# A hybrid decoder layer: where the attention heads' merge operands and softmax sums are loaded

## Chip, cores and metric

The kernel runs on one core of a Trainium2 chip, in one launch. The metric is the device time of one execution in microseconds (us). Engines are named as in the profile: PE is TensorE, DVE VectorE, ACT ScalarE, POOL GpSimd, SP SyncE, which issues most of the DMAs.

## The reference

One layer on x of 1 x 1024 x 1024 in float32: a half-step SwiGLU FFN, a mixer of two branches, a second half-step FFN, a final norm. Only the end of the mixer matters here:

```python
o_dn = rmsnorm(gated_delta_rule(...), dn_out_norm) * silu(dn_z)      # branch A, 8 heads of 128
# branch B: 8 heads; each query keeps its top-256 causal keys
logits = q_lat . c_sel * 128**-0.5 + rel_bias                        # masked
p = softmax(logits)
o_sa = (p . c_sel) @ w_uv                                            # per head, 128 wide
merged = sigmoid(gate_a) * o_dn + sigmoid(gate_b) * o_sa
x = x + merged @ w_o
```

## The kernel before

Every product is made of three matmuls on split operands (`mm3`, lines 139 to 141): a value is cast to a high part and the rest is kept as a low part (line 111 casts on ScalarE, line 112 subtracts on VectorE or GpSimd). The matrices are float32r, the tokens stand in eight blocks of 128.

Before the attention, the delta-rule stage writes its normed output, transposed per head, to `odd` in DRAM, and the gates are written to `zgd` (branch A's gate times silu of z) and `gbd` (the tanh of branch B's gate). In the attention stage `attn_head` runs for eight heads. Per head it goes through four groups g in the order 0, 1, 3, 2, each with two query blocks. For a block it makes the logits (`pl`), adds a mask or a near-bias tile `nb` made on GpSimd (line 1309) while it takes the maximum `a_mx` on VectorE (line 1322), and exponentiates on ScalarE (line 1327), which also gives the row sums `a_sum`. Then the probabilities are transposed on TensorE (`pp`), split into `ph` and `plo` (lines 1338, 1339), and multiplied with the values `vh`, `vl` into the one PSUM bank `pao`; ScalarE copies that into `osa` (line 1344).

After group 1 and after group 2 a half of the head (512 queries) is complete and `merge` is called. It takes the reciprocal of the sums (line 1364), issues three loads from SP (`od`, `zg`, `gb`, line 1369, one buffer each), writes the reciprocals to DRAM (`a_rd`, line 1378) and loads them back spread over all partitions (`a_rb`, line 1380, also SP, which waits there until `a_rd` has landed). The second part of the merge, `done`, multiplies `od` by `zg` on GpSimd (1383), `osa` by `a_rb` and by 1 + `gb` on VectorE (1384, 1385) and adds both into `merged` on GpSimd (1386). It is held back in the list `outs`: for the half after group 1 until the end of group 3, for the half after group 2 until the end of the next head's group 1. `issue_after(dve.ins)` puts its VectorE instructions behind the last `plo` of that group.

`ahead` in group 1 makes the next head's queries and keys (`attn_qk`, line 1288 casts, 1289 subtracts, tile `p`) at a raised priority. `attn_values` makes the values of a pair of heads every second head, in one tile `vh` and one `vl`, from the weights `w_uv`. All weight loads share the two slots of `w_raw`, which are free again when ScalarE has cast and GpSimd has subtracted (tile `wa`).

The order of the instructions on each engine is found by a list scheduler at build time, which takes the ready instruction of the highest priority, by the order of the program unless `high_priority` raises it; each engine and each DMA queue then runs its own list in order. The tiles of a tag share its buffers (`bufs`), and an instruction that writes a buffer waits for the readers of the tile before.

Of the kernel before, what the change touches and what calls it, by code (L numbers as in the profile page):

```python
# [10 lines left out]
F32 = mybir.dt.float32  # L11
F32R = mybir.dt.float32r
# [3 lines left out]
ALU = mybir.AluOpType  # L16
# [4 lines left out]
P = 128  # L21
D = 1024
S = 1024
NK = D // P
NT = S // P
D_FF = 2816
NF = D_FF // P
H = 8
# [42 lines left out]
class Layer:  # L71
# [1188 lines left out]
    def attn_values(self, pair, p, ps):  # L1260
        nc = self.nc
        wh, wl = self.attn_weights(self.I["w_uv"][0][:, 2 * pair:2 * pair + 2, :].rearrange("r h d -> r (h d)"), 256, p, "wuv")
        vh = p.tile([P, NT, 256], F32R, name="vh", tag="vh", bufs=1)
        vl = p.tile([P, NT, 256], F32R, name="vl", tag="vl", bufs=1)
        for t in range(0, NT, 2):
            pv = ps.tile([P, 2, 256], F32, name="pav", tag="qk")
            for i in range(2):
                for k in range(2):
                    lh, ll = (x[2 + k][t // 4][:, ts((t + i) % 4, P)] for x in self.lat)
                    self.mm3(pv[:, i, :], lh, ll, wh[:, k, :], wl[:, k, :], k == 0, k == 1)  # L1270
            nc.scalar.copy(vh[:, t:t + 2, :], pv)
            nc.vector.tensor_sub(vl[:, t:t + 2, :], pv, vh[:, t:t + 2, :])
        return vh, vl

    def attn_qk(self, hd, p, ps):
# [19 lines left out]
    def attn_head(self, hd, p, ps, qk, values, merged, ahead):  # L1295
        nc = self.nc
        near = self.near_tile(p, hd)
        (qh, ql), (kh, kl) = qk
        vh, vl = values
        hv = slice((hd % 2) * P, (hd % 2) * P + P)  # L1300
        sums = self.stat.tile([P, NT], F32, name="a_sum")
        osa = p.tile([P, S], F32, name="osa", tag="osa", bufs=2)
        for g in (0, 1, 3, 2):
            probs = []
            for b in (2 * g, 2 * g + 1):
                W = (b + 1) * P
                n_near = min(W, 256)
                nb = p.tile([P, 256], F32, name="nb", tag="nb", bufs=4)
                nc.gpsimd.tensor_add(nb[:, 256 - n_near:], near[:, 256 - n_near:], self.mask[b][:, W - n_near:W])
                s = self.slot(("w_hi", "w_lo")[b % 2])  # L1310
                mx = self.stat.tile([P, 4], F32, name="a_mx", tag="a_mx", bufs=3)
                m = 0
                for n0 in range(0, W, 512):
                    n1 = min(W, n0 + 512)
                    pl = ps.tile([P, 512], F32, name="pl", tag="lg")
                    self.mm3(pl[:, 0:n1 - n0], qh[b // 4][:, ts(b % 4, P)], ql[b // 4][:, ts(b % 4, P)], kh[n0 // 512][:, 0:n1 - n0],
                             kl[n0 // 512][:, 0:n1 - n0], True, True)
                    for a0, a1 in ((n0, min(n1, W - n_near)), (max(n0, W - n_near), n1)):
                        if a1 <= a0:
                            continue  # L1320
                        add = nb[:, a0 - W + 256:a1 - W + 256] if a0 >= W - n_near else self.mask[b][:, a0:a1]
                        nc.vector.tensor_tensor_reduce(s[:, a0:a1], pl[:, a0 - n0:a1 - n0], add, 1.0,
                                                       mx[:, m - 1:m] if m else -3.0e38, ALU.add, ALU.max, accum_out=mx[:, m:m + 1])
                        m += 1
                nm = self.stat.tile([P, 1], F32, name="a_nm", tag="a_nm", bufs=3)
                nc.vector.tensor_scalar_mul(nm, mx[:, m - 1:m], -1.0)
                nc.scalar.activation(s[:, 0:W], s[:, 0:W], AF.Exp, bias=nm, accum_out=sums[:, b:b + 1])
                probs.append(s)
            po = ps.tile([P, 512], F32, name="pao", tag="ao")
            for j in range(0, 2 * g + 2, 2):  # L1330
                pt = ps.tile([P, 512], F32, name="pp", tag="pt")
                blocks = [(j, 0), (j, 1), (j + 1, 0), (j + 1, 1)] if j < 2 * g else [(j, 0), (j, 1), (j + 1, 1)]
                n = len(blocks) * P
                for i, (jj, b) in enumerate(blocks):
                    nc.tensor.transpose(pt[:, ts(i, P)], probs[b][:, ts(jj, P)], self.ident)
                ph = p.tile([P, 512], F32R, name="ph", tag="ph", bufs=3)
                pl_ = p.tile([P, 512], F32R, name="plo", tag="plo", bufs=3)
                nc.scalar.copy(ph[:, 0:n], pt[:, 0:n])
                dve = nc.vector.tensor_sub(pl_[:, 0:n], pt[:, 0:n], ph[:, 0:n])
                for i in range(2):  # L1340
                    a, b = (0, 256) if i == 0 else (256, n)
                    out = po[:, 0:256] if b - a == 256 else po[:, 128:256]
                    self.mm3(out, vh[:, j + i, hv], vl[:, j + i, hv], ph[:, a:b], pl_[:, a:b], j + i == 0, j + i == 2 * g + 1)
            nc.scalar.copy(osa[:, ts(g, 256)], po[:, 0:256])
            if g == 1:
                ahead()
            for late in self.outs:
                late[0] -= 1
            while self.outs and self.outs[0][0] == 0:
                with self.tc.issue_after(dve.ins):  # L1350
                    self.outs.pop(0)[1]()
            if g in (1, 2):
                out = self.merge(hd, g // 2, sums, osa, p, ps, merged)
                if hd == H - 1 and g == 2:
                    out()
                else:
                    self.outs.append([g, out])

    def merge(self, hd, h, sums, osa, p, ps, merged):


        nc = self.nc
        r = self.stat.tile([P, 4], F32, name="a_r")
        nc.vector.reciprocal(r, sums[:, ts(h, 4)])
        nc.vector.tensor_scalar_mul(r, r, 0.5)
        od, zg, gb = (p.tile([P, 512], F32, name=n, tag=n, bufs=1) for n in ("od", "zg", "gb"))
        v = ts(h, 512)
        for x, src in ((od, self.odd[hd][:, v]), (zg, self.zgd[hd][:, v]), (gb, self.gbd[hd][:, v])):
            nc.sync.dma_start(x, src)
        if hd == H - 1 and h == 1:  # L1370
            rb = ps.tile([P, 512], F32, name="a_rp", tag="pt")
            for t in range(4):
                d = p.tile([P, P], F32, name="a_d", tag="near", bufs=2)
                nc.vector.tensor_scalar_mul(d, self.ident, r[:, t:t + 1])
                nc.tensor.matmul(rb[:, ts(t, P)], lhsT=self.ones, rhs=d, start=True, stop=True)
        else:
            rd = self.dram.tile([512], F32, name="a_rd", tag="a_rd", bufs=2)
            nc.sync.dma_start(rd.rearrange("(t i) -> i t", i=P), r)
            rb = p.tile([P, 512], F32, name="a_rb", tag="a_rb", bufs=1)
            nc.sync.dma_start(rb, rd.partition_broadcast(P))  # L1380

        def done():
            nc.gpsimd.tensor_mul(od, od, zg)
            nc.vector.tensor_mul(osa[:, v], osa[:, v], rb)
            nc.vector.scalar_tensor_tensor(osa[:, v], gb, 1.0, osa[:, v], ALU.add, ALU.mult)
            nc.gpsimd.tensor_add(merged[:, v], od, osa[:, v])

        return done


    def out_proj(self, m, ps, after_tile, after_half):
# [137 lines left out]
    def mixer(self, hs):  # L1529

        nc = self.nc
        ms = ExitStack()
        with ExitStack() as km:
            keep = self.pool(km, "keep", 1)
            self.masks(keep)
            with ExitStack() as ss:
                ps = Banks(self.psum, g=(0, 1), u=(2, 3), t=(4, 5, 6, 7), d=(4, 5, 6, 7))
# [29 lines left out]
                with ExitStack() as c2:  # L1567
                    sp = self.pool(c2, "blocks", 1)
                    blocks = [self.solve_blocks(k, sp, ps) for k in range(2)]
                    with ExitStack() as c3:  # L1570
                        p = self.pool(c3, "qkv", 1)
# [26 lines left out]
                ps = Banks(self.psum, g=(0,), u=(2,), pq=(4, 5), pv=(1, 3), pn=(6, 7), po=(1, 3), qk=(0, 2))  # L1598
# [14 lines left out]
            with ExitStack() as c:  # L1613
                ps = Banks(self.psum, qk=(0, 1), lg=(2, 4, 5), pt=(6, 7), ao=(3,))
                p = self.pool(c, "attn", 1)
                mlp = self.pool(c, "merged_raw", 1)
                raw = [mlp.tile([P, S], F32, name=f"mr{k}", tag=f"mr{k}") for k in range(NK)]
                qk = self.qk

                def ahead():  # L1620
                    if len(qk) < H:
                        with self.tc.high_priority(offset=AHEAD):
                            qk.append(self.attn_qk(len(qk), (p, "wqk", 2), ps))

                for i in range(H):
                    if i % 2 == 0:
# [58 lines left out]
```

## Time and profile before

| | us |
|---|---|
| median of 3 runs | 2654.05 (2652.68 to 2655.29) |
| profiled execution, its own time | 2654.08 |
| its span in the trace | 2652.1 |
| TensorE matmuls busy | 2519.1 (95%) |
| VectorE, ScalarE, GpSimd busy | 1737.9, 1198.3, 970.9 |

Times in the trace are counted from the start of the span; the attention stage lies between about 1600 and 1880 us. The granted clock is the share of TensorE's full clock that the chip granted, as a mean over a stretch. "Idle before" or a wait is the time for which an engine's next instruction was held, put down to the work that released it; "issue" means that the profile shows no releaser. The chain of waits follows back, from the last instruction of a stretch, what released each step. "To landing" is the time from the issue of a DMA to its completion. SPq is SP's queue, PEld TensorE's weight loads.

### The profile page before, as it was taken

The numbers are of one execution on the slowest core, as the hardware profiler recorded it, in microseconds if no ns is written. First come the engines' busy times: TensorE is split into PE (matmuls) and PEld (weight loads), VectorE is DVE, ScalarE is ACT, GpSimd is POOL, SyncE is SP. The second block draws the span as 40 slices with busy tenths as digits, with TensorE's granted clock in tenths as the row PEclk, the third lists the DMA queues.
The fourth block names the chain that finished last, engine by engine and source line by source line (L and its number), as shares of the span: only waits on it lengthen the run. The fifth ranks groups of instructions, "written<-read, shape, count | busy, mean of one in ns | idle before, by whom it ended". The sixth has DMA issues, their size and how long they took to land.

```text
span 2652.1 us, 36132 instructions
## 1 busy us (share of the span) xinstructions
PE 2519.1 (95%) x12526; PEld 2054.9 (77%) x12526; DVE 1737.9 (66%) x3424; ACT 1198.3 (45%) x2338; POOL 970.9 (37%) x748
## 2 busy tenths in 40 slices
PE   6999999999999899989999999779898999999998
PEld 5788888888787688777778778678776888888886
DVE  7655555676555677999566866566668555546676
ACT  6444344333434665544368446445434434434333
POOL 5555444343434233332100002333446545543340
PEclk8999999999999899999999999889998999999999
DMA  5443346753444155445633323333632344347642
GB/s 168 136 143 129 113 146 219 255 194 101 120 114 122 41 140 139 115 124 123 200 124 116 124 82 74 82 76 78 200 111 94 102 143 143 127 150 263 224 151 75
DMA packets 375607, 356.67 MB, mean 134 GB/s; under 512 B 95417, under 2 KB 279553, under 8 KB 374401
## 3 DMA queue, kind: packets, MB, share of 16 engines
q1 hardware_dynamic: 371840, 348.60, 42.1%
q10 hardware_dynamic: 2304, 4.20, 0.4%
q0 software_dynamic: 1280, 1.57, 0.3%
q8 instruction: 99, 1.62, 0.3%
q14 instruction: 84, 0.68, 0.1%
HBM read 238.28 MB, written 116.01 MB: 134 GB/s over the span
## 4 chain that ended last, share of the span: by engine, by line
PE 40%; DVE 9%; DMA 6%; issue 2%; ACT 1%; POOL 1%; SPq 0%; DVEq 0%; POOLq 0%; ACTq 0%
PE pst L139 7%; PE pst L141 7%; PE pst L140 7%; PE pin L141 2%; PE pin L139 2%; PE pin L140 2%; DVE sb_p L1034 2%; DMA a_rd<-a_r 2%; DMA od<-odd 1%; PE pn L1221 1%; PE po L1230 1%; PE pv L1216 1%; DVE cv_y L923 1%; PE pq L1211 1%; PE pwo L141 1%
## 5 line engine op out<-in xcount | busy, mean ns | idle before, releaser
L140 PE MATMUL pst<-p,w_hi 128*128 128x512 f32 x992 | 392.1, 395 | 8.6 <-DVE p L112 8.5
L139 PE MATMUL pst<-p,w_hi 128*128 128x512 f32 x992 | 393.2, 397 | 4.1 <-ACT p L111 2.3
L141 PE MATMUL pst<-p,w_hi 128*128 128x512 f32 x992 | 391.3, 395 | 0.5 <-DVE w_hi L112 0.5
L139 PE MATMUL pin<-p,w_hi 128*128 128x512 f32 (+1 forms) x848 | 342.1, 405 | 6.0 <-DVE cv_y L923 4.2
L111 ACT CAST w_hi<-w_raw 128x512 fp32r<-128x512 f32 (+3 forms) x294 | 204.1, 695 | 311.7 <-PE pst L141 135.8
L140 PE MATMUL pin<-p,w_hi 128*128 128x512 f32 (+1 forms) x848 | 340.5, 402 | 0.5 <-DVE p L112 0.5
L141 PE MATMUL pin<-p,w_lo 128*128 128x512 f32 (+1 forms) x848 | 340.8, 402 | 0.0
L112 DVE TENSOR_TENSOR w_lo<-w_raw,w_lo 128x512 fp32r<-128x512 f32 (+1 forms) x196 | 188.3, 963 | 167.2 <-ACT w_lo L111 165.6
L140 PE MATMUL pst<-p,w_lo 128*128 128x512 f32 x744 | 292.7, 394 | 3.7 <-DVE p L112 3.7
L141 PE MATMUL pst<-p,w_lo 128*128 128x512 f32 x744 | 292.2, 393 | 1.2 <-DVE w_lo L112 1.2
L139 PE MATMUL pst<-p,w_lo 128*128 128x512 f32 x744 | 290.6, 396 | 0.5 <-ACT c L360 0.5
L140 PEld LDWEIGHTS pst<-p,w_hi 128*128 128x128 f32 x992 | 188.3, 190 | 53.9 <-DVE p L112 12.9
L139 PEld LDWEIGHTS pst<-p,w_hi 128*128 128x128 f32 x992 | 188.8, 190 | 47.3 <-ACT p L111 3.5
L141 PEld LDWEIGHTS pst<-p,w_hi 128*128 128x128 f32 x992 | 188.5, 190 | 43.0 <-DVE w_hi L112 1.3
L111 ACT CAST w_lo<-w_raw 128x512 fp32r<-128x512 f32 (+1 forms) x200 | 115.7, 582 | 207.4 <-PE pst L141 97.8
L139 PEld LDWEIGHTS pin<-p,w_hi 128*128 128x128 f32 (+1 forms) x848 | 161.6, 191 | 42.7 <-DVE cv_y L923 4.5
L141 PEld LDWEIGHTS pin<-p,w_lo 128*128 128x128 f32 (+1 forms) x848 | 161.5, 190 | 37.7 <-issue 3.8
L140 PEld LDWEIGHTS pin<-p,w_hi 128*128 128x128 f32 (+1 forms) x848 | 161.6, 191 | 37.5 <-issue 4.0
L373 DVE TENSOR_TENSOR c<-c,pst 128x512 f32<-128x512 f32 x132 | 89.9, 682 | 150.9 <-PE pst L141 118.1
L112 POOL TENSOR_TENSOR w_lo<-w_raw,w_hi 128x1024 fp32r<-128x1024 f32 (+1 forms) x43 | 107.0, 2488 | 199.4 <-ACT w_hi L111 189.4
L140 PEld LDWEIGHTS pst<-p,w_lo 128*128 128x128 f32 x744 | 140.7, 189 | 35.1 <-DVE p L112 4.9
L141 PEld LDWEIGHTS pst<-p,w_lo 128*128 128x128 f32 x744 | 140.7, 189 | 33.5 <-DVE w_lo L112 2.1
(427 smaller groups left out, 5393.8 us busy)
## 6 DMA issues: line engine op xcount, KB each, us to landing
p<-mixd SPq DMA_DIRECT2D x144, 256.0 KB, 5.4
w_raw<-in_w_in_dram SPq DMA_DIRECT2D x52, 512.0 KB, 4.1
w_raw<-in_ffn_wg_dram SPq DMA_DIRECT2D x44, 512.0 KB, 3.6
w_raw<-in_ffn_wu_dram SPq DMA_DIRECT2D x44, 512.0 KB, 4.0
mixd<-t_hi SPq DMA_DIRECT2D x72, 256.0 KB, 4.3
mixd<-t SPq DMA_DIRECT2D x72, 256.0 KB, 3.8
w_raw<-in_ffn_wd_dram SPq DMA_DIRECT2D x48, 384.0 KB, 4.1
actd<-c SPq DMA_DIRECT2D x70, 256.0 KB, 2.0
```

The costliest lines, as they stand in the source:

```text
L111: self.nc.scalar.copy(hi, raw)
L112: self.pin((self.nc.vector if engine == "vector" else self.nc.gpsimd).tensor_sub(lo, raw, hi))
L139: mm(ps, lhsT=wh, rhs=rh, start=first, stop=False, **kw)
L140: mm(ps, lhsT=wh, rhs=rl, start=False, stop=False, **kw)
L141: mm(ps, lhsT=wl, rhs=rh, start=False, stop=last, **kw)
L373: nc.vector.tensor_add(c[i, h], c[i, h], bank["y" if m == 1 else "z"])
L923: nc.vector.scalar_tensor_tensor(y[:, n:512], pps[h][:, 0:512 - n], cw[:, j:j + 1], y[:, n:512], ALU.mult, ALU.add)
L1034: nc.vector.tensor_mul(v, T[:, 0:i, 0:i].rearrange("p j c -> p c j"), L[:, None, 0:i, i].to_broadcast([P, i, i]))
L1211: nc.tensor.matmul(pq[:, i, :], lhsT=kq[:, h, ts(c, P)], rhs=old[:, h, :], start=True, stop=True)
L1216: nc.tensor.matmul(pv[r, i, :], lhsT=X[r, h, :], rhs=vb[r, h, :], start=True, stop=True)
L1221: nc.tensor.matmul(pn[:, i, :], lhsT=kd[r, h, :], rhs=vn[r, h, :], start=True, stop=True)
L1230: nc.tensor.matmul(po[r, i, :], lhsT=at[r, h, :], rhs=vn[r, h, :], start=True, stop=True)
```

## The change

The product of `od` and `zg` becomes a generator of its own, `other_branch`. It loads a whole head's `odd` straight into `merged` and a whole head's `zgd` into one buffer of 1024, from SP, at the end of group 3 of the head before (for the first head ahead of all heads), and multiplies both halves on GpSimd at the end of its own head's group 0. `merge` becomes a generator of three steps, each one group later than the one before: reciprocal, `gb` load and `a_rd` write; then the `a_rb` load, issued from ScalarE's queue behind that group's copy into `osa`; then the two VectorE passes and the addition into `merged`. So the half after group 1 ends with group 2 in place of group 3; the half after group 2 ends with the next head's group 1, as before. `osa` is two tiles of 512 instead of two of 1024, `gb` and `a_rb` have two buffers each, `vh` and `vl` four tiles each, and the very last addition is VectorE's.

```diff
@@ attn_values
-        vh = p.tile([P, NT, 256], F32R, name="vh", tag="vh", bufs=1)
-        vl = p.tile([P, NT, 256], F32R, name="vl", tag="vl", bufs=1)
+        vh, vl = ([p.tile([P, 2, 256], F32R, name=n, tag=f"{n}{t}", bufs=1) for t in range(NT // 2)] for n in ("vh", "vl"))
...
-            nc.scalar.copy(vh[:, t:t + 2, :], pv)
-            nc.vector.tensor_sub(vl[:, t:t + 2, :], pv, vh[:, t:t + 2, :])
+            nc.scalar.copy(vh[t // 2], pv)
+            nc.vector.tensor_sub(vl[t // 2], pv, vh[t // 2])
@@ attn_head
-        osa = p.tile([P, S], F32, name="osa", tag="osa", bufs=2)
         for g in (0, 1, 3, 2):
+            if g in (0, 3):
+                osa = p.tile([P, 512], F32, name="osa", tag="osa", bufs=2)
...
-            nc.scalar.copy(osa[:, ts(g, 256)], po[:, 0:256])
-            if g == 1:
-                ahead()
-            for late in self.outs:
-                late[0] -= 1
-            while self.outs and self.outs[0][0] == 0:
-                with self.tc.issue_after(dve.ins):
-                    self.outs.pop(0)[1]()
+            act = nc.scalar.copy(osa[:, ts(g % 2, 256)], po[:, 0:256])
+            ahead(hd, g)
+            with self.tc.issue_after(dve.ins), self.tc.issue_after(act.ins):
+                for out in self.outs:
+                    next(out, None)
+            self.outs = self.outs[-1:]
             if g in (1, 2):
                 out = self.merge(hd, g // 2, sums, osa, p, ps, merged)
+                next(out)
+                self.outs.append(out)
                 if hd == H - 1 and g == 2:
-                    out()
-                else:
-                    self.outs.append([g, out])
+                    for _ in out:
+                        pass
@@ merge
-        od, zg, gb = (p.tile([P, 512], F32, name=n, tag=n, bufs=1) for n in ("od", "zg", "gb"))
+        gb = p.tile([P, 512], F32, name="gb", tag="gb", bufs=2)
         v = ts(h, 512)
-        for x, src in ((od, self.odd[hd][:, v]), (zg, self.zgd[hd][:, v]), (gb, self.gbd[hd][:, v])):
-            nc.sync.dma_start(x, src)
+        nc.sync.dma_start(gb, self.gbd[hd][:, v])
...
             nc.sync.dma_start(rd.rearrange("(t i) -> i t", i=P), r)
-            rb = p.tile([P, 512], F32, name="a_rb", tag="a_rb", bufs=1)
-            nc.sync.dma_start(rb, rd.partition_broadcast(P))
-
-        def done():
-            nc.gpsimd.tensor_mul(od, od, zg)
-            nc.vector.tensor_mul(osa[:, v], osa[:, v], rb)
-            nc.vector.scalar_tensor_tensor(osa[:, v], gb, 1.0, osa[:, v], ALU.add, ALU.mult)
-            nc.gpsimd.tensor_add(merged[:, v], od, osa[:, v])
-
-        return done
+            yield
+            rb = p.tile([P, 512], F32, name="a_rb", tag="a_rb", bufs=2)
+            nc.scalar.dma_start(rb, rd.partition_broadcast(P))
+        yield
+        nc.vector.tensor_mul(osa, osa, rb)
+        nc.vector.scalar_tensor_tensor(osa, gb, 1.0, osa, ALU.add, ALU.mult)
+        (nc.vector if last else nc.gpsimd).tensor_add(merged[:, v], merged[:, v], osa)
+
+    def other_branch(self, hd, p, merged):
+
+        nc = self.nc
+        zg = p.tile([P, S], F32, name="zg", tag="zg", bufs=1)
+        nc.sync.dma_start(merged, self.odd[hd])
+        nc.sync.dma_start(zg, self.zgd[hd])
+        yield
+        for h in range(2):
+            nc.gpsimd.tensor_mul(merged[:, ts(h, 512)], merged[:, ts(h, 512)], zg[:, ts(h, 512)])
@@ mixer
-                def ahead():
-                    if len(qk) < H:
+                others = [self.other_branch(k, p, raw[k]) for k in range(H)]
+                next(others[0])
+
+                def ahead(hd, g):
+                    if g == 0:
+                        next(others[hd], None)
+                    elif hd + 1 < H and g == 1:
                         with self.tc.high_priority(offset=AHEAD):
-                            qk.append(self.attn_qk(len(qk), (p, "wqk", 2), ps))
+                            qk.append(self.attn_qk(hd + 1, (p, "wqk", 2), ps))
+                    elif hd + 1 < H and g == 3:
+                        next(others[hd + 1])
```

## Rows read from the trace of the kernel before

**Rows 1.** Stretches: bounds, length, busy (count) of PE, PEld, DVE, ACT, POOL; clock, DMA

```profile
1600.00:1620.00 20.00, 15.67 (x78) 12.50 (x76) 10.04 (x43) 14.04 (x40) 8.69 (x12) 0.74 0.47 133
...
1660.00:1680.00 20.00, 14.76 (x96) 13.28 (x94) 11.64 (x46) 8.02 (x21) 4.48 (x7) 0.83 0.15 46
1690.00:1720.00 30.00, 17.98 (x90) 15.03 (x89) 9.31 (x25) 8.53 (x21) 10.53 (x12) 0.72 0.34 89
1720.00:1760.00 40.00, 38.59 (x272) 35.02 (x270) 31.48 (x107) 23.12 (x55) 16.33 (x21) 1.00 0.31 67
...
1770.00:1790.00 20.00, 8.52 (x27) 6.90 (x28) 6.07 (x18) 5.02 (x13) 6.09 (x6) 0.59 0.32 79
...
1810.00:1860.00 50.00, 40.39 (x267) 35.60 (x265) 31.85 (x101) 24.40 (x55) 15.51 (x17) 0.95 0.38 80
1860.00:1880.00 20.00, 16.06 (x79) 12.96 (x80) 19.68 (x38) 13.49 (x26) 8.87 (x7) 0.86 0.28 80
```

**Rows 2.** Waits of the engines from 1600 to 1880: total us, times, longest us

```profile
POOL od L1383 <- DMA od<-odd: 61.4, 8, 14.7
...
POOL od L1383 <- issue: 50.1, 6, 15.5
ACT wa L111 <- DMA w_raw<-in_w_uv_dram: 36.5, 3, 17.7
...
DVE osa L1384 <- DMA a_rb<-a_rd: 26.7, 9, 6.3
...
PE pqk L139 <- DVE p L1289: 22.2, 4, 9.1
...
PE pl L139 <- DVE a_mx L1322: 9.9, 3, 5.1
```

**Rows 3.** Waits of SP's queue from 1595 to 1885: total us, times, longest us

```profile
SPq L1369 <- POOL od L1383: 91.0, 15, 12.5
SPq L1380 <- DMA a_rd<-a_r: 85.2, 12, 11.2
```

**Rows 4.** Chain of waits from 1650 to 1730: start us, length us, what

```profile
1683.33 10.89 DMA od<-odd
...
1698.59 3.21 DMA od<-odd
...
1703.23 0.69 POOL wa L112
1703.94 9.19 DMA w_raw<-in_w_uv_dram
...
1715.83 0.43 PE pqk L140
...
1721.08 0.23 PE pqk L140
```

**Rows 5.** Line 1378, the 15 writes of the sums

```profile
DMA to landing us min/median/max: 9.9/11.5/13.1
```

**Rows 6.** Line 1380, the loads of the spread sums: issue (ns min/median/max), landing

```profile
L1380 SPq DMA_DIRECT2D a_rb<-a_rd x15: 319/320/371, 1628.2 to 1871.3; - x15
...
DMA to landing us min/median/max: 4.2/4.9/6.3
```

**Rows 7.** Timeline of VectorE: reciprocal of head 3's second half

```profile
1737.05 0.18 DVE L1364 RECIPROCAL a_r<-a_sum 128x4 f32<-128x4 f32 x1
```

**Rows 8.** Timeline of ScalarE: last copy of head 3, first two of head 4

```profile
1751.23 0.39 ACT L1344 COPY osa<-pao 128x256 f32<-128x256 f32 x1
...
1754.06 0.38 ACT L1344 COPY osa<-pao 128x256 f32<-128x256 f32 x1
...
1760.68 0.35 ACT L1344 COPY osa<-pao 128x256 f32<-128x256 f32 x1
```

**Rows 9.** Instructions on tile `osa`: ns min/median/max

```profile
L1385 DVE SCALAR_TENSOR_TENSOR osa<-gb,osa x16: 679/692/1759, 1641.6 to 1895.9; 128x512 f32<-128x512 f32 x16
L1386 POOL TENSOR_TENSOR mr<-od,osa x16: 1269/1288/1748, 1642.7 to 1896.7; 128x512 f32<-128x512 f32 x16
```

More of the change, by code (lines that the diff above doesn't have):

```diff
@@ L1342, in attn_head @@
                     out = po[:, 0:256] if b - a == 256 else po[:, 128:256]
-                    self.mm3(out, vh[:, j + i, hv], vl[:, j + i, hv], ph[:, a:b], pl_[:, a:b], j + i == 0, j + i == 2 * g + 1)
-            nc.scalar.copy(osa[:, ts(g, 256)], po[:, 0:256])
-            if g == 1:
-                ahead()
-            for late in self.outs:
-                late[0] -= 1
-            while self.outs and self.outs[0][0] == 0:
-                with self.tc.issue_after(dve.ins):
-                    self.outs.pop(0)[1]()
+                    self.mm3(out, vh[j // 2][:, i, hv], vl[j // 2][:, i, hv], ph[:, a:b], pl_[:, a:b], j + i == 0, j + i == 2 * g + 1)
+            act = nc.scalar.copy(osa[:, ts(g % 2, 256)], po[:, 0:256])
[4 more added lines that the diff above has]
+            self.outs = self.outs[-1:]
             if g in (1, 2):
                 out = self.merge(hd, g // 2, sums, osa, p, ps, merged)
+                next(out)
+                self.outs.append(out)
                 if hd == H - 1 and g == 2:
-                    out()
-                else:
-                    self.outs.append([g, out])
+                    for _ in out:
+                        pass
     def merge(self, hd, h, sums, osa, p, ps, merged):
@@ L1365, in merge @@
         nc.vector.tensor_scalar_mul(r, r, 0.5)
-        od, zg, gb = (p.tile([P, 512], F32, name=n, tag=n, bufs=1) for n in ("od", "zg", "gb"))
+        gb = p.tile([P, 512], F32, name="gb", tag="gb", bufs=2)
         v = ts(h, 512)
-        for x, src in ((od, self.odd[hd][:, v]), (zg, self.zgd[hd][:, v]), (gb, self.gbd[hd][:, v])):
-            nc.sync.dma_start(x, src)
-        if hd == H - 1 and h == 1:
+        nc.sync.dma_start(gb, self.gbd[hd][:, v])
+        last = hd == H - 1 and h == 1
+        if last:
             rb = ps.tile([P, 512], F32, name="a_rp", tag="pt")
```

## The prediction

> **What bounds the kernel now.** I read the table of stretches first, over the attention stage, because only its code changes. In the table a stretch's loss is its length less TensorE's busy time multiplied by the granted clock, that is, the work done as if at full clock. The reader is to see where that loss sits [rows 1]: 20 - 15.67 x 0.74 = 8.4 us at 1600, 20 - 14.76 x 0.83 = 7.7 at 1660, 30 - 17.98 x 0.72 = 17.1 at 1690, 1.4 at 1720, 20 - 8.52 x 0.59 = 15.0 at 1770, 50 - 40.39 x 0.95 = 11.6 at 1810, 20 - 16.06 x 0.86 = 6.2 at 1860: 67 us. In the good stretch, 1720 to 1760, TensorE is busy 38.59 of 40 at full clock, while VectorE needs only 31.48 and ScalarE 23.12. So the stage is TensorE's when nothing stands still, and the holes are waits.
>
> Next the waits of the stage. GpSimd stands 61.4 us for `od` and 50.1 more ahead of the same multiplication without a named releaser; ScalarE stands 36.5 us for the `w_uv` load; VectorE stands 26.7 us for `a_rb` [rows 2]. TensorE itself stands 22.2 us, nearly all in waits of up to 9.1, for VectorE's `p` and 9.9 us for `a_mx`. Third the waits of SP's own queue: 91.0 us for the multiplication `od` (a load that needs the single `od` and `zg` buffers back) and 85.2 us at L1380, where the load of the spread sums waits for the sums to land in DRAM [rows 3]. Everything behind these on SP waits too.
>
> The chain shows how these meet in the hole at 1690 [rows 4]. GpSimd's weight subtraction (1703.23) is queued behind the `od` multiplication; only then is the `w_raw` slot free, the `w_uv` load is issued at 1703.94 and needs 9.19 us, and ScalarE, in order, has `p` behind that cast. TensorE stands, and then runs at the lower level: 0.43 us from one 512-column matmul to the next at 1715.83, 0.23 us at 1721.08 [rows 4]. These are the 1.2 and 2.4 GHz levels; the 0.72 of this stretch and the 0.59 of 1770 [rows 1] are mixtures.
>
> **The change part by part.**
>
> *Operands loaded a head ahead.* 16 `od` and 16 `zg` loads of 256 KB become 8 and 8 of 512 KB: the same bytes. `od` needs no buffer back, as it goes straight into `merged`; `zg` still has one buffer, freed by GpSimd's two multiplications at the head's first group, a whole unit sequence ahead of the next use. The 16 multiplications stay, as do the additions of 1.29 us [rows 9], so GpSimd's work is unchanged, with 16.33 of 40 us busy in the good stretch [rows 1]. What goes is the wait ahead of them and with it what stood behind: weight subtractions and `nb` tiles. This opens the holes at 1690 and 1770 and part of that at 1810.
>
> At 1690 and 1770 the `w_uv` load remains, but is issued when its slot is really free. It was issued 1703.94 - 1698.59 = 5.4 us after the `od` load that GpSimd was held by, and GpSimd had been held by the earlier `od` load of 10.89 us before that [rows 4]. Between all of the loss back (17.1 and 15.0) and about a third (6 and 5, if the load keeps its 9.19 us and ScalarE's cast stays where it is) I take 14 and 12, nearer the full end, since the good stretch carries the same kind of work at 1.4 lost in 40.
>
> *Sums from ScalarE's queue, a unit later.* SP loses 15 issues of 0.32 us and with them the wait of 85.2 us. ScalarE gains 15 issues; at SP's price of 0.32 that is 4.8 us in a stage where it has 17 of 40 us free: nothing, unless it waits. It would wait for `a_rd`, which lands 9.9 to 13.1 us after issue [rows 5]. In the steady heads the reciprocal of head 3's second half starts at 1737.05 [rows 7]; with 11.5 us and about 0.5 for scale and issue the sums are there at 1749.1, at the latest measured landing 1750.7. ScalarE reaches its new place, behind the copy of head 4's first group, at 1754.06 + 0.38 = 1754.4 [rows 8]. The cover is 4 to 5 us; without it each microsecond short costs ScalarE up to 15 us over the stage.
>
> For the first half of a head VectorE's multiplication moves from the end of the third group to the end of the fourth. That removes the wait of 6.3 us at 1660 [rows 2], which TensorE paid with 5.1 us (longest `a_mx` wait) and a restart at low clock: of 7.7 I take 6 back, bounds 3 and 7.7. In the hole at 1810 `a_rb` waits and one `od` wait meet: of 11.6 I take 8, bounds 3 and 11.6. For the second half the multiplication stays where it was, but the load now starts behind a fixed copy: 1754.4 + 4.9 [rows 6] = 1759.3, against a copy of the second group at 1760.68 [rows 8], ahead of which the multiplication stands. That is a wait of 0 to 3 us for each of 7 heads, about 9 us of VectorE in all at 1.3 each; waits this short fall into its free fifth, so I charge TensorE 3 (bounds 0 and 9).
>
> *`osa` in halves.* Two tiles of 512 in place of two of 1024. The copy of the next head's first group now needs the tile of this head's first half back, and this comes only after two VectorE passes and GpSimd's addition: 0.69 + 0.69 + 1.29 = 2.67 us [rows 9], behind the last `plo` of the fourth group. From the copy of the fourth group to that of the next first group there are 1754.06 - 1751.23 = 2.83 us [rows 8]. So this is the new wait: with anything queued ahead on VectorE or GpSimd, ScalarE's copy stands, `pao` has one bank, and TensorE's next accumulation waits behind it. Bounds: 0, and 3 us in each of 7 heads = 21; I take 4, as the nearest row has the two almost equal.
>
> *Start.* Eight targets of `od` are free from the outset, so their loads may be issued together with the first heads' weights. The worst that one such load can meet is a landing like `od`'s 10.89 us; once, so bounds 0 and 11, and I take 3.
>
> *Values in four tiles, `gb` and `a_rb` with two buffers, the last addition on VectorE.* The four tiles let the first value pairs be written before the last group's accumulations are over; in the good stretch, which holds one change of pair, TensorE lost 1.4 in 40 [rows 1], so I take 0, bounds 0 and 1.4. The buffers belong to the moves above. The last addition (1.29 on GpSimd, 0.69 on VectorE) lies beside output-projection matmuls: 0.
>
> The losses at 1600 (ScalarE's end of the delta stage) and 1860 (VectorE 19.68 of 20 busy, with the splits of `merged`) stay [rows 1].
>
> *Sum:* 6 + 14 + 12 + 8 = 40 gained, 3 + 4 + 3 = 10 lost: 30 us. From the profiled execution's 2654.08 us (span 2652.1 and 2.0 outside it; the median is 2654.05, the same) this gives 2624 us.
>
> **The rivals.**
>
> *The weight load stays late.* `w_uv` still lands in some 9 us, and ScalarE's cast still holds `p`. For it: 9.19 us here, and 10.89 for `od` at 1683, against 3.21 for the `od` load at 1698 [rows 4]. Against it: the slot comes free earlier. Then 1690 and 1770 give 8 and 6 in place of 14 and 12: 2636 us, chance 0.17.
>
> *The start costs its bound:* the operand loads bunch in front of the first heads' weights, 11 in place of 3, with a second such meeting at most: 2632 to 2643 us, chance 0.08.
>
> *The spread sums land behind the next sums' write.* A load that was issued while an `a_rd` was under way took 9.19 and 10.89 us, in place of 3.21 without [rows 4]; in the new order the next `a_rd` is under way when ScalarE issues `a_rb`. If the second halves' `a_rb` land in 9.2 in place of 4.9 us [rows 6], VectorE waits 4.3 x 7 = 30 us more, and at TensorE's share in the hole at 1660 (5.1 of 6.3) this is 24: 2648 us, chance 0.08. Against it: a steady head's next write would land about when `a_rb` does anyway.
> The Trainium skill's page "DMA: Bandwidth & Descriptors", section "Queues, rings and completion order", has a rule for this: a transfer's completion mark is written only after every earlier write of that DMA engine, whichever queue it came from. By that rule ScalarE's queue is no way around a slow write, and the time is this rival's 2648; the trace agrees in the 9.19 and 10.89 us, all on SP's queue, but has no load on ScalarE's behind an `a_rd`.
>
> *ScalarE stands at the new issue: slower.* If the closed-up order brings the reciprocal so near that the cover of 4 to 5 us is gone, the 85 us of waiting on SP [rows 3] move into ScalarE's queue, with `ph`, `p` and the copies behind them. It decides from 3.3 us short in each of 15 merges: 50 us, of which ScalarE's free two fifths hide 20, and the other 30 are the whole gain. At 5 short, 75 less 30 hidden, it is 2624 + 45 = 2669. Against it: the 17 us between reciprocal and copy. Chance 0.07.
>
> *Nothing moves:* the holes were held by something else, and the next engine's waits fill them. Against it: VectorE, the next, has a fifth free where TensorE is at 96%. 2652, chance 0.05.
>
> *All of it comes back:* 7.7 + 17.1 + 15.0 + 11.6 + 1.4 = 53 with costs near 2: 2603, chance 0.13.
>
> **How the numbers follow.** The forecast, 2624 with its own range of 2612 to 2634, has the remaining 0.42. A measurement of this kernel can tell 0.2%, 5.3 us, from no change. Faster by more: 0.42 + 0.17 + 0.08 + 0.13, and 0.05 of the spread-sums case, which lies on that edge: 0.85. Within: its other 0.03 and the case in which nothing moves: 0.08. Slower: 0.07. The range of 2600 to 2651 leaves out the slower case, half of the one where nothing moves, and a little below: about 0.14.
>
> **What would show it.** Right: GpSimd's wait ahead of its multiplications falls from 111 us to under 30; no wait of SP for `a_rd`; ScalarE's waits for `w_uv` under 5 us each; the granted clock at 1.00 where 1690 and 1770 now show 0.72 and 0.59; the stage some 30 us shorter and the stages after it unchanged. Wrong: waits of ScalarE's queue at the `a_rb` issue, of its copies into `osa` for GpSimd's addition, or of VectorE for `a_rb` beyond 20 us in all; GpSimd again standing for `zg` with `nb` tiles behind it.

## The result

The changed kernel takes 2672.48 us (median of 8 runs, 2665.39 to 2681.46) against 2653.03 for the kernel before beside it (8 runs, 2647.43 to 2655.29): ratio 1.0080, interval 1.0065 to 1.0094. It is 0.8% slower. The forecast was 2624, range 2600 to 2651: wrong in sign, and out of the range.

The execution that was profiled is the slowest of the eight (2681.46, span 2679.8), so its span lies 27.7 us above that of before, 8 more than the medians do; the holes below are read for their place and cause, and the sizes of effects are taken from the timed ratios.

First the table of stretches of the changed kernel, with the columns of [rows 1] and mostly its bounds.

```profile
1690.00:1720.00 30.00, 27.68 (x180) 24.72 (x179) 21.34 (x65) 18.32 (x43) 12.53 (x16) 0.94 0.31 58
...
1770.00:1790.00 20.00, 20.00 (x123) 18.18 (x123) 12.75 (x35) 10.04 (x21) 6.75 (x8) 0.93 0.20 55
1810.00:1860.00 50.00, 37.68 (x241) 34.67 (x240) 29.11 (x92) 22.62 (x52) 11.86 (x15) 0.86 0.19 45
...
1600.00:1880.00 280.00, 227.65 (x1415) 202.03 (x1413) 164.38 (x529) 143.03 (x334) 96.47 (x113) 0.90 0.35 77
1880.00:2100.00 220.00, 196.71 (x848) 157.48 (x849) 140.43 (x190) 84.72 (x139) 96.10 (x63) 0.93 0.38 122
...
1670.00:1690.00 20.00, 6.78 (x34) 6.27 (x35) 5.64 (x21) 4.63 (x11) 9.57 (x10) 0.66 0.60 105
1760.00:1780.00 20.00, 14.66 (x91) 13.27 (x90) 12.23 (x37) 8.53 (x17) 3.40 (x4) 0.83 0.22 45
```

The same table of the kernel before, for the two long stretches and for three that [rows 1] leaves out:

```profile
1600.00:1880.00 280.00, 231.24 (x1435) 203.68 (x1433) 178.26 (x550) 145.14 (x338) 98.91 (x114) 0.89 0.33 79
1880.00:2100.00 220.00, 209.49 (x916) 168.72 (x915) 144.78 (x185) 89.66 (x146) 109.61 (x73) 0.96 0.42 138
...
1670.00:1690.00 20.00, 16.63 (x107) 15.04 (x108) 15.61 (x47) 10.97 (x24) 3.80 (x4) 0.83 0.37 96
1760.00:1780.00 20.00, 12.69 (x70) 10.56 (x70) 6.55 (x12) 4.47 (x10) 4.64 (x6) 0.84 0.35 67
...
1880.00:1900.00 20.00, 20.00 (x109) 17.13 (x108) 12.40 (x14) 7.54 (x11) 9.77 (x7) 1.00 0.57 166
```

With the loss as in the prediction (length less busy times clock), the two holes that the change aimed at are nearly closed within their old bounds: 1690 goes from 17.1 to 30 - 27.68 x 0.94 = 4.0, 1770 from 15.0 to 1.4. But much of the loss now lies beside them: 20 - 6.78 x 0.66 = 15.5 at 1670, where the kernel before lost 6.2, and 7.8 at 1760, where it lost 9.3 (as one stretch, 1760 to 1790 goes from 17.2 to 8.1). The 50 us from 1810 lose 17.6 in place of 11.6. From 1600 to 1880 the sum is 280 - 227.65 x 0.90 = 75.1, against 74.2 before: nothing gained. After 1880 another 37.1 go, against 18.9, and the stage had begun 5 us later (SP's write of `odd` goes out at 1610.11 in place of 1604.76). Most of the 18 lie at the end of the heads, in two stretches where TensorE was busy and at full clock before:

```profile
1880.00:1890.00 10.00, 3.49 (x8) 2.84 (x9) 5.31 (x10) 5.76 (x12) 2.87 (x2) 0.60 0.42 124
1890.00:1900.00 10.00, 7.61 (x38) 6.16 (x37) 9.34 (x15) 2.01 (x3) 2.22 (x2) 0.88 0.00 0
```

Now the waits of the changed kernel's engines from 1600 to 1880 (total us, times, longest), beside [rows 2], and of SP's queue, beside [rows 3].

```profile
POOL nb L1309 <- DVE a_mx L1322: 88.6, 26, 14.8
...
DVE osa L1382 <- DMA a_rb<-a_rd: 43.9, 10, 14.2
...
POOL mr L1394 <- DMA zg<-zgd: 19.6, 5, 9.1
...
ACT osa L1344 <- POOL mr L1384: 12.1, 1, 12.1
...
ACT wa L111 <- DMA w_raw<-in_w_uv_dram: 9.9, 3, 5.2
```

```profile
SPq L1367 <- DVE osa L1383: 72.4, 9, 13.2
```

What was to go is gone: GpSimd's 111.5 us ahead of its multiplications are 19.6, SP waits no more for `a_rd`, ScalarE's wait for `w_uv` falls from 36.5 to 9.9. In their place VectorE waits 43.9 us for `a_rb` in place of 26.7, and others wait for VectorE: SP with its `gb` load for the buffer that VectorE's second pass frees, and GpSimd for `a_mx`. Of GpSimd's 88.6 us, 69.9 remain in the much faster run with the short write below, so most of this wait is not what made the kernel slower.

Why `a_rb` comes late is seen in the timeline: the writes of the sums on SP (L1377), the loads that spread them on ScalarE's queue (L1380), and VectorE's pass behind each (L1382; in brackets what it stood).

```profile
1737.92 0.37 SPq L1377 DMA_DIRECT2D a_rd<-a_r  x1
...
1755.49 0.37 SPq L1377 DMA_DIRECT2D a_rd<-a_r  x1
...
1759.47 0.33 ACTq L1380 DMA_DIRECT2D a_rb<-a_rd  x1
...
1768.17 0.69 DVE L1382 TENSOR_TENSOR osa<-osa,a_rb 128x512 f32<-128x512 f32 x1 [5.57 <-DMA a_rb<-a_rd]
...
1775.64 0.33 ACTq L1380 DMA_DIRECT2D a_rb<-a_rd  x1
...
1778.82 0.69 DVE L1382 TENSOR_TENSOR osa<-osa,a_rb 128x512 f32<-128x512 f32 x1 [0.84 <-DMA a_rb<-a_rd]
...
1869.24 0.37 SPq L1377 DMA_DIRECT2D a_rd<-a_r  x1
...
1872.14 0.33 ACTq L1380 DMA_DIRECT2D a_rb<-a_rd  x1
...
1884.69 0.69 DVE L1382 TENSOR_TENSOR osa<-osa,a_rb 128x512 f32<-128x512 f32 x1 [8.23 <-DMA a_rb<-a_rd]
```

Loads and writes pair in their order. The load at 1759.47 spreads the sums that were written from 1737.92; 4.0 us before it the next write was issued, and it lands 8.69 us later. The load at 1775.64, with no write issued in the 14.9 us before it (the nearest was at 1760.69), lands in 3.2. So it is through the stage: of the 14 loads up to 1880, eight were issued 2.9 to 8.6 us behind a write that was not their own, and land 5.7 to 12.5 us after their issue, 10.5 to 16.7 after that write's; the other six land in 3.1 to 4.0. Two of the eight, those at 1759.47 and 1826.80, also have a further write 1.2 us behind them. The last of the eight lands 12.53 after 1872.14. Behind VectorE's pass stand the eight splits of `merged` (L112, 8.06 us in the chain), and TensorE's `pwo` stands 9.1 us for them: the stretch from 1880 above.

The packets of ScalarE's queue (q10) tell whether the data of a load were late or only its landing. For the load at 1826.80 all packets had run by 1830.1 (first line: the window 1826.8 to 1830.1; packets, MB, share), but VectorE was released only at 1838.01. For the load at 1872.14 none ran up to 1882, where SP's queue (q1) is the only one with packets (last line: 1872.1 to 1882): there the data themselves went late.

```profile
q10 hardware_dynamic: 144, 0.26, 23.8%
```

```profile
1826.80 0.33 ACTq L1380 DMA_DIRECT2D a_rb<-a_rd  x1
...
1838.01 0.69 DVE L1382 TENSOR_TENSOR osa<-osa,a_rb 128x512 f32<-128x512 f32 x1 [8.07 <-DMA a_rb<-a_rd]
```

```profile
q1 hardware_dynamic: 55, 0.11, 17.1%
```

The hole at 1670 begins with a late load too, of `zg`. The chain there shows 9.05 us in which GpSimd's gate multiplication has no `zg` yet (the row says "issue", but this is the 9.1 us for `zg` in the waits above), then its addition, then ScalarE's copy, which needs that addition for its half of `osa`, and only behind the copy the issue of `a_rb`, which lands in 3.36. SP had issued that `zg` load at 1669.34, 6.3 us behind the write at 1663.08. The `zg` load at 1640.85, 1.0 us behind the write at 1639.84, took 13.10 us; the one at 1662.69, with no write in the 22 us before it, 3.59.

```profile
1640.85 13.10 DMA zg<-zgd
...
1662.69 3.59 DMA zg<-zgd
...
1669.31 9.05 issue
...
1678.40 2.48 POOL mr L1394 x2
...
1681.26 1.23 POOL mr L1384
...
1682.52 0.02 ACT osa L1344
...
1682.58 3.36 DMA a_rb<-a_rd
...
1685.96 1.57 DVE osa L1382
```

### The profile page after: what moved, and what is told of

Its sections match the earlier page's. It is cut to its first block, busy times and chain, and to the rows that moved or that the text cites. A ratio compares the mean times of both kernels' runs of the same rounds, so it can differ in the third digit from the quotient of the medians.

```text
span 2679.8 us, 36089 instructions
## 1 busy us (share of the span) xinstructions
PE 2528.8 (94%) x12526; PEld 2063.4 (77%) x12526; DVE 1735.3 (65%) x3425; ACT 1199.9 (45%) x2338; POOL 970.9 (36%) x747
## 4 chain that ended last, share of the span: by engine, by line
PE 40%; DVE 9%; DMA 5%; issue 2%; ACT 2%; POOL 1%; SPq 0%; DVEq 0%; ACTq 0%; POOLq 0%
PE pst L139 7%; PE pst L141 7%; PE pst L140 7%; PE pin L141 2%; PE pin L140 2%; PE pin L139 2%; DMA a_rb<-a_rd 2%; DVE sb_p L1034 2%; PE po L1230 1%; PE pn L1221 1%; PE pv L1216 1%; DVE cv_y L923 1%; PE pq L1211 1%; PE pwo L139 1%; PE pwo L141 1%
## 5 line engine op out<-in xcount | busy, mean ns | idle before, releaser
L112 DVE TENSOR_TENSOR w_lo<-w_raw,w_lo 128x512 fp32r<-128x512 f32 (+1 forms) x196 | 190.2, 973 | 168.4 <-ACT w_lo L111 166.7
L139 PEld LDWEIGHTS pin<-p,w_hi 128*128 128x128 f32 (+1 forms) x848 | 162.5, 192 | 43.3 <-DVE cv_y L923 4.5
L112 POOL TENSOR_TENSOR w_lo<-w_raw,w_hi 128x1024 fp32r<-128x1024 f32 (+1 forms) x43 | 106.8, 2485 | 201.9 <-ACT w_hi L111 194.7
```

Source lines behind the costliest of these rows:

```text
L112: self.pin((self.nc.vector if engine == "vector" else self.nc.gpsimd).tensor_sub(lo, raw, hi))
L139: mm(ps, lhsT=wh, rhs=rh, start=first, stop=False, **kw)
```

## The experiments

The theory (A): the write of the sums, 512 pieces of 4 bytes with 9.9 to 13.1 us to landing [rows 5], is what loads land behind, on whichever queue. Rival (B): GpSimd's multiplications that run ahead, and the half tiles of `osa` behind them. Rival (A2): the issue behind ScalarE's copy costs by itself. All ratios are to the kernel before on the same chip, 2644.86 to 2646.98 us there. In the first batch:

**Short write.** Each partition's four sums are written as one run of 16 bytes, and VectorE reads the spread tile with a stride.

```
-            nc.sync.dma_start(rd.rearrange("(t i) -> i t", i=P), r)
+            nc.sync.dma_start(rd.rearrange("(i t) -> i t", t=4), r)
...
-        nc.vector.tensor_mul(osa, osa, rb)
+        o3 = osa.rearrange("p (t i) -> p t i", t=4)
+        nc.vector.tensor_mul(o3, o3, rb.rearrange("p (t i) -> p t i", t=4) if last else rb.rearrange("p (i t) -> p t i", t=4))
```

> The changed kernel with one edit: the sums are written to DRAM as 128 runs of 16 bytes instead of 512 of 4 bytes, and VectorE reads the spread sums with a stride of four. Theory A (the spread sums, issued from ScalarE, land behind the next sums' write of 10 to 13 us, and VectorE stands for them: 52.2 us in the changed kernel): the write lands in under 5 us, VectorE's wait for a_rb falls from 52.2 to under 15 us, and the time falls by 20 to 30 us from 2672 to 2642 to 2652. Theory B (the gate multiplications run ahead of their heads and hold GpSimd, and the half-size osa tiles pass that on to ScalarE and TensorE): the time stays within 6 us of 2672.

2618.08 us, ratio 0.9897 (0.9871 to 0.9923): 1.8% below the changed kernel's ratio, more than any theory gave. VectorE's waits, and the landings of the writes and of the spread loads (min, median, max):

```profile
DVE osa L1383 <- DMA a_rb<-a_rd: 8.8, 8, 4.9
```

```profile
DMA to landing us min/median/max: 1.4/1.8/7.6
...
DMA to landing us min/median/max: 3.0/3.3/3.8
```

The queue, the units and the half tiles are those of the changed kernel, and the waits are gone, although VectorE's strided pass takes 1.09 us in place of 0.69. That the write makes these loads late is shown. How much of the change's loss is the write's is not, until the kernel before has had the same edit (below).

**Spread loads back on SP** (`nc.scalar.dma_start(rb, ...)` becomes `nc.sync.dma_start(rb, ...)`).

> The changed kernel with one edit: the spread sums are loaded from SP's queue instead of ScalarE's, at the same place of the program. Theory A in its strict form (a load completes only behind an earlier slow write, whichever queue it came from): landings of 8 to 12 us stay where a write is under way, VectorE's wait stays above 35 us, and the time is within 8 us of 2672. Theory A2 (what is late is the issue, fixed behind ScalarE's copy): the load goes as soon as the sums have landed, VectorE's wait falls to about the 27 us of the kernel before, and the time to about 2655. Theory B: no change, 2672.

2648.64, ratio 1.0012 (0.9996 to 1.0028). SP waits for the write again, longer than before, and what stands behind it on SP is late again:

```profile
SPq L1380 <- DMA a_rd<-a_r: 140.0, 15, 12.9
```

```profile
ACT wa L111 <- DMA w_raw<-in_w_uv_dram: 24.5, 3, 11.9
```

VectorE's own wait for `a_rb` is 0.2 us here. Theory A's figures for this run failed: on SP each spread load goes out when its own write has landed, and the other writes are 21 us or more back. A2's figures were nearer. So ScalarE's queue is what turned a draw into a loss. That could be A (there the load meets the next write) or A2; the short write on SP, below, decides.

**Operands alone**: the kernel before with only `other_branch` and its calls.

> The kernel before with one part of the change: the product of od and zg is loaded a head ahead and straight into merged; sums, osa and values as before. Theory B (this part is what costs): slower than 2653, at 2660 or more, with GpSimd standing for zg loads early in the stage. Theory A (the sums are what costs, the operands' part works as forecast): the two waits of ScalarE for w_uv at 1695 and 1766 of 17 us each are gone, and the time is 2625 to 2640.

2646.89, ratio 1.0004 (0.9991 to 1.0017): nothing, and neither theory's figure. GpSimd no longer stands for `od` (25.7 us for `zg` are left), and `w_uv` is late all the same, 31.9 us in place of 36.5. SP's queue shows why, and the chain what came of it:

```profile
1710.36 0.39 SPq L1376 DMA_DIRECT2D a_rd<-a_r  x1
1710.80 0.50 SPq L1256 DMA_DIRECT2D w_raw<-in_w_uv_dram  x1
```

```profile
1710.80 12.11 DMA w_raw<-in_w_uv_dram
```

The weights go out 0.44 us behind a write and land with it.

**Multiplications held** (`ahead(hd, g)` inside `issue_after` of the unit's last addition to `nb`; full write).

> The changed kernel with one edit: the two gate multiplications of a head stay behind the last near-bias tile of that head's first group on GpSimd, so that they no longer run ahead. Theory B: the stop at 1670 (ScalarE's copy 12.1 us behind GpSimd's addition, VectorE 14.3 us for a_rb) goes, and the time falls by 12 to 20 us, to 2652 to 2660. Theory A: the other waits for a_rb stay and the time is within 6 us of 2672.

2673.72, ratio 1.0114 (1.0083 to 1.0145). The `zg` waits are down to 1.8 us, VectorE waits 43.3 us for `a_rb` as it did, and the time is no better: B, as the whole cause, falls.

The second batch. **The kernel before with the short write alone.**

> The kernel before, with the sums written as 128 runs of 16 bytes in place of 512 of 4, and nothing of the change. Theory A (loads that are issued while the sums are on their way land with them, in the kernel before as in the changed one): the landing of a_rd falls from 9.9-13.1 us to 1.4-2, the wait of the w_uv load's cast from 12 us a time to under 5, and the time from 2645 to 2615-2632. Theory C (the short write only takes back the harm that the change itself did): 2638-2645, within 0.3% of before. If it reaches the 2618 of the changed kernel with the short write, the change itself is worth nothing even then; if it stays 8 or more above, that difference is the change's worth once the write is short.

2606.98, ratio 0.9851 (0.9829 to 0.9873): theory A, with a time below its range. Most of the waits that the prediction had read as GpSimd's, `od`'s and SP's were this write's:

```profile
POOL od L1383 <- DMA od<-odd: 16.8, 7, 5.2
...
POOL od L1383 <- issue: 9.6, 5, 2.9
...
ACT wa L111 <- DMA w_raw<-in_w_uv_dram: 4.5, 3, 2.6
```

It is also 11 us faster than the changed kernel with the same write (12 by the ratios, whose intervals just touch): with the short write in both, the change costs time.

**Values in one tile each again**, in the changed kernel.

> The changed kernel with the values in one tile each again. Theory A gives the four tiles no part in the loss: ratio 1.006 to 1.011 to before, as the changed kernel itself (on this chip 2661 to 2674). The rival, that the four tiles are what lost (the split of the values interleaved otherwise with the units), puts it at before, 2645 plus or minus 5. If the four tiles gain what the prediction took for them (a part of the 14 us of the hole at 1690), it comes out 5 to 14 us slower than the changed kernel, 2672 to 2688.

2681.08, ratio 1.0127 (1.0102 to 1.0152): slower than the changed kernel, by 12 us as the ratios stand, and out of theory A's range: the four tiles' worth there, which the prediction had at 0.

**Short write, spread loads on SP.**

> The changed kernel with the short write of the sums, and the loads that spread them (a_rb) issued from SP instead of ScalarE. Theory A: with the write short, the place of the issue matters little, 2613 to 2623 (the changed kernel with the short write: 2618.1). Theory A2 (an issue behind ScalarE's copies has a price of its own, as the 24 us between the changed kernel and its run with these loads on SP could also mean): below 2610. If SP's waits for a_rd, 12.9 us a time with the long write, shrink to 2-4 us and still hold up the loads behind them: 2622 to 2630.

2619.78, ratio 0.9904 (0.9868 to 0.9939), the 2618.08 of ScalarE's queue within both intervals. The four runs spread from 2613.30 to 2631.62, so a price of up to some 9 us could hide here, but not the 18 us between the two queues with the full write, and A2's figure, below 2610, failed. With the short write the queue shows no price, so its price with the full write is A's.

**Three half tiles of `osa`** (`bufs=3`), full write.

> The changed kernel with three half tiles of osa instead of two. Theory A: the 12.1 us wait of ScalarE's copy for GpSimd's addition goes, but the spread loads still land 8 to 12 us late behind the next write, so the time stays within 6 us of the changed kernel, ratio 1.005 to 1.012 (2659 to 2676 on this chip). Theory B (the loss is ScalarE standing for a free half tile): 10 to 15 us faster than the changed kernel, 2650 to 2660.

2668.16, ratio 1.0086 (1.0057 to 1.0115). The 12 us hole of ScalarE's copy is gone and the time stays: VectorE still stands 38.9 us for `a_rb`.

Third batch, to split the change. **Values alone**, and **values with the short write**, both in the kernel before.

> The kernel before with the values in four tiles and nothing else of the change. If the four tiles are worth what they were in the changed kernel: 2634 to 2642. If the values' weight load, which lands 11 to 12 us late behind the write of the sums, sets the holes at 1690 and 1770 however the values are tiled: 2643 to 2650, no change.

2634.46, ratio 0.9953 (0.9933 to 0.9973): 11 us faster, the only part of the change that was seen to gain by itself (the merge's steps were not run alone).

> The kernel before with the short write of the sums and the values in four tiles. In the changed kernel the four tiles were worth about 9 us (2681 with one tile, 2672 with four). Theory V1 (they help only where something else comes late; with the short write TensorE is busy 198 of 200 us from 1620 to 1720 and 1740 to 1800, so nothing is left to help): 2603 to 2610, as with one tile (2607.0). Theory V2 (they help by themselves): 2595 to 2601.

2601.66, ratio 0.9825 (0.9806 to 0.9844): between the two theories, 5 us below one tile, with the intervals overlapping. It is the fastest kernel of the study.

**Changed kernel, short write, multiplications held**; then also three half tiles.

> The changed kernel with the short write, and GpSimd's gate multiplications held behind the additions of the unit that issues them, as in the run that held them with the long write. Theory D (the 11 us by which the changed kernel stays behind the one before, 2618 against 2607 with the short write in both, are GpSimd's multiplications of eight heads run ahead of the additions that the first head waits for): 2603 to 2612, and no hole of TensorE at 1650 to 1665. Rival (the half tiles of osa or the wider loads at the start): 2614 to 2622.

> The same with three half tiles of osa. Theory D: within 4 us of the run with two half tiles, since ScalarE's copy waited for GpSimd's addition 2.6 us once with the short write. If the half tiles are what is left of the loss: 5 to 10 us faster than that run. Below 2605 it would be the fastest of all, and the change would be worth something once the write is short.

2612.72, ratio 0.9875 (0.9856 to 0.9893), and 2616.27, 0.9882 (0.9862 to 0.9902). Both lie within the interval of the run without (0.9897), so D is not shown; the half tiles cost nothing that could be measured.

Last, **the change without the merge's new steps** (operands and values only), with the full and the short write; and the changed kernel with short write, multiplications held, and the merge's steps not held behind ScalarE's copy.

> The kernel before with the operands loaded a head ahead and the values in four tiles, with the merge's steps (write and spread loads of the sums together on SP, whole osa tiles) as before: the change without its second part. If the parts add up, the operands' 0 and the values' -11: 2632 to 2638. The changed kernel, about 2667 on this chip, would then owe some 30 us to the merge's steps alone, of which 19 to 24 went when the spread loads were given back to SP. Rival: operands and values together cost what neither does alone: 2645 or more.

2642.78, ratio 0.9987 (0.9973 to 1.0000): between the two cases.

> The same with the short write of the sums. If the operands cost nothing here too: 2599 to 2605, as without them (2601.7), and the 16 us to the changed kernel with the short write (2618.1) are the merge's steps again. If the operands' wide loads and the multiplications of eight heads run ahead are that loss: 2611 to 2619.

2614.36, ratio 0.9887 (0.9867 to 0.9908): the upper case. Beside values alone, the operands cost 12.7 us here by the medians and 16 by the ratios; with the full write 8.3 (2642.78 less 2634.46) or 9. The tables of stretches of values alone and of operands with values, both with the short write:

```profile
1600.00:1640.00 40.00, 35.67 (x214) 30.67 (x213) 25.93 (x90) 26.81 (x65) 15.45 (x22) 0.91 0.36 95
1640.00:1660.00 20.00, 20.00 (x146) 18.64 (x145) 15.33 (x52) 11.92 (x28) 8.28 (x10) 1.00 0.32 91
1660.00:1680.00 20.00, 19.86 (x140) 17.88 (x140) 18.69 (x61) 14.48 (x35) 10.14 (x12) 1.00 0.30 92
```

```profile
1600.00:1640.00 40.00, 35.46 (x203) 30.66 (x204) 24.51 (x90) 25.39 (x59) 22.16 (x27) 0.91 0.72 227
1640.00:1660.00 20.00, 19.82 (x152) 18.74 (x151) 16.43 (x53) 11.63 (x26) 14.13 (x12) 1.00 0.43 129
1660.00:1680.00 20.00, 15.17 (x98) 13.80 (x97) 15.00 (x43) 9.69 (x24) 13.65 (x14) 0.91 0.33 90
```

With the operands, the DMA engines are 0.72 busy from 1600 in place of 0.36, and GpSimd works 14.13 of 20 us at 1640 in place of 8.28: all 16 multiplications start between 1615.1 and 1668.4. TensorE then misses 20 - 15.17 x 0.91 = 6.2 us at 1660. But the execution that was profiled is the fastest of its run, 2606.66, only 3.6 us above the profiled one of values alone (2603.10), so these tables cannot place the 12.7 us of the medians.

> The changed kernel with the short write and the multiplications held (2612.7), and the merge's steps held behind VectorE's last subtraction of the unit alone, not behind ScalarE's copy too. If the order behind the copy costs (VectorE's passes and the spread loads are issued later by the attention sum that the copy waits for): 2602 to 2608. If not: 2609 to 2616.

2623.02, ratio 0.9917 (0.9898 to 0.9936): neither case; the order behind the copy does not cost, and seems to save some 10 us (the two intervals lie just apart).

The ratios to the kernel before, side by side:

| | sums in 4-byte pieces | in 16-byte runs |
|---|---|---|
| before | 1 | 0.9851 |
| + values | 0.9953 | 0.9825 |
| + operands | 1.0004 | |
| + values, operands | 0.9987 | 0.9887 |
| whole change, spread loads on SP | 1.0012 | 0.9904 |
| whole change | 1.0080 | 0.9897 |

The last two rows are the test of the cause. ScalarE's queue costs 18 us beside the full write (1.0080 less 1.0012), and nothing that shows beside the short one. So most of the 0.8% by which the change lost is this queue meeting this write. What it does not explain is why the rest of the change gained nothing: on SP's queue it stands at 1.0012 with the full write and, against the kernel before with the same short write, 14 us behind (0.9904 less 0.9851).

## Why the prediction was wrong

**The write of the sums was seen and not followed.** The prediction had its 9.9 to 13.1 us, priced it as SP's wait at the next load and as a cover for ScalarE's queue, and took all else that was slow near it (`od` 10.89, `w_uv` 9.19) as separate things. The short write alone takes 40 us from the kernel before: that is more than half of the 67 us of loss that it counted in [rows 1].

**Two steps failed.** The step that made the change slower is the term for `a_rb`: for the second halves "0 to 3 us for each of 7 heads", 3 us with bounds 0 and 9, and for the first halves no wait at all, with the 6.3 us at 1660 booked as gone. It stood on a landing of 4.9 us [rows 6], measured where SP had just waited for the write and none was under way. In the new order one is, for eight loads of 14, four of them of first halves. VectorE waits 35.2 us for the second halves' seven loads, where the term allowed about 9 (14.25 of it in the hole at 1670, where the issue was late and not the landing), and 17.0 us for the first halves'. The last wait alone holds the output projection. In the timed runs the merge's steps, with the half tiles of `osa`, cost 25 us (0.9987 to 1.0080), 18 of them the move to ScalarE's queue. The other failed step is the gain of 14 and 12 put to the operands: alone they gave 0 (1.0004). ScalarE's wait for `w_uv` stayed at 31.9 us with `od` out of the way, and fell to 4.5 with the short write.

**The right rival was named and mispriced twice.** "The spread sums land behind the next sums' write" is what happened. Its chance, 0.08, came from the argument that the next write lands about when `a_rb` does anyway; the write at 1755.49, 4.0 us ahead of the load, had most of its time still to go when the load was issued. Its price, 24 us, kept every gain and charged only the second halves, at 9.2 us; the loads took up to 12.53, and the one at the end, an 8.2 us wait of VectorE, cost TensorE (10 - 3.49 x 0.60) + (10 - 7.61 x 0.88) = 11.2 us with the splits and the low clock behind it, more than the 5.1 of 6.3 that the price went by.
The rule of the Trainium skill that the prediction set beside it ("DMA: Bandwidth & Descriptors", "Queues, rings and completion order": the completion mark follows every earlier write of that DMA engine, across queues) fits the load at 1826.80, whose packets had all run some 8 us before VectorE was released. It does not cover the load at 1872.14, of which no packet had run 9.8 us after its issue; what held those data is open.
The same page of the Trainium skill, section "Rules for kernel authors", says that a last dimension that isn't contiguous becomes one descriptor per element, and to rearrange it. That rule spoke of this write and was not weighed; 2606.98 against 2646.84 agrees with it.

**The terms 14 and 12** seem to come as sizes, 13.1 and 13.6 within their bounds in the changed kernel, but 9.3 of the first stand again at 1670 and part of the second at 1760, and they did not come from the edit that they were put to. With the operands alone `w_uv` left just behind a write; it came early only when SP no longer waited, and what that gained came back as `a_rb`. The 6 and 8 for the holes at 1660 and 1810 did not come: one moved to 1670, the other grew.

**ScalarE's cover** held: no wait of its queue at the issue shows among its waits, so the rival that ended slower was not how it became slower.

**`osa` in halves** (4 us) showed one wait of 12.1 us, but three tiles did not change the time. **The start** (3 us, bound 11): the eight pairs of loads do bunch, as that rival had it, and the operands cost 8 to 16 us beside the values, but no run shows that the bunching is what costs. **The four tiles** were no 0 with bound 1.4: 11 us alone. The good stretch showed what TensorE lost where all went well; the tiles count where the values come late.

**Open:** why the operands cost nothing alone but 8 to 16 us beside the four tiles, and where that time lies; what the merge's steps would do without the rest of the change; and how the write holds a load, since one load's data had gone and were reported late, and another's went late.

## What to carry to other kernels

When several different loads are slow in the same places, look for the transfer that is under way in all of them, and shorten that one, before their order is changed. Moving a load to another engine's queue takes its wait from one engine; it does not take the load out from behind a write in pieces of 4 bytes. A landing time holds for the order in which it was measured: ask what will be in flight at the new place.

## What was not expected of the hardware

Written as 512 pieces of 4 bytes, the 2 KB of sums take 9.9 to 13.1 us to land; as 128 runs of 16 bytes, 1.4 to 3.9 with a median of 2.5 in the kernel before, and up to 7.6 in the changed one. The load that spreads them lands in 3.0 to 4.2 there. A 256 KB load issued 0.44 us behind the write in small pieces took 12.11 us; with the short write the loads of these weights have a median of 2.9 (the last column; ahead of it the KB of each).

```profile
w_raw<-in_w_uv_dram SPq DMA_DIRECT2D x3, 256.0 KB, 2.9
a_rd<-a_r SPq DMA_DIRECT2D x15, 2.0 KB, 2.5
```
